# Storing two tiles of a matmul's output: SyncE's six partitions move to GpSimd, and the transfers are cut anew

## Chip, cores and metric

The kernel runs on one core of one Trainium2 chip. The metric is the device time of the kernel in microseconds; the time before is the median of three runs. The core moves data with 16 DMA engines. SyncE (SP) and GpSimd (POOL) each have a queue of transfers to them: in the profile q1, "hardware_dynamic", is SyncE's and q0, "software_dynamic", is GpSimd's.

## What is computed

```python
x          (16, 512, 1024) float32
weight     (1024, 768)     float32
scale      0.1
add_value  (16, 512, 768)  float32
out = (scale * np.matmul(x, weight) + add_value).astype(np.float32)
```

Flattened, that is 8192 rows of x against one weight matrix.

## The kernel before

The 8192 rows are cut into 64 tiles of 128 rows, four blocks of `R = 16`. A block has 2048 consecutive rows, 16 to each partition, so tile t of a block is row t of each partition. A run of n neighbouring tiles of a block is then n x 3072 consecutive bytes per partition of the output, and a transfer of it has one long packet per partition.

- **SyncE** (`sync_engine`) issues the transfers of a list written out by hand, `STREAM`, in its order: "w" loads the weight, "x" loads tiles of x into the 16 places of `xs`, "a" loads tiles of add_value into the 32 places of `ao`, "o" stores tiles from `ao`. Ahead of an entry it waits for what the entry needs (`need`): a load into a place that has been used waits for that place to be free, a store waits on `made`, VectorE's count of finished tiles. Later entries wait behind an entry that waits. The very last store, tiles 60 to 63, stands at the end of the kernel.
- **ScalarE and GpSimd** (`mover`) cast x to bf16, each half of the partitions, and lay it out in `va`.
- **VectorE** (`vector_engine`) casts the weight once, transposes `va` into `xt` and finishes two tiles at a time: `ao = scale * mm + ao`.
- **TensorE** multiplies tile by tile, eight weight pieces for each, into PSUM (`mm`).

Tiles 8 and 15 of the first block are stored apart from their neighbours. The stream stores tiles 0 to 7 with ("o", 0, 8) and 9 to 14 with ("o", 9, 6). The pair, places 8 and 15 of `ao` (`PAIR`, a slice with step 7), is stored by `store_pair`, which takes a range of partitions and has two rows of 3072 bytes for each. The 128 partitions are divided: SyncE's entry ("pair", 8, 8) stores the six in `BY_SP`; GpSimd stores the others in three transfers, `BY_POOL`, between its second and third turn over the 16 places of `xs`, once tile 15 is made. `TURN_AT` places that between two loops of casts.

Tiles 40 to 47 of add_value are loaded over places 8 to 15, so SyncE's "a" entry for them, line 129, waits for both parts of the pair: `pair_sem` for SyncE's transfer, `aside_sem` for GpSimd's three, each counting 16 to a transfer. Behind that entry in the stream stand x 48 to 55 (line 116) and the stores of tiles 16 to 31 (line 147). Line 93 is the transfer in `store_pair`, line 258 the last store.

Of the kernel before, what the change touches and what calls it, by code (L numbers as in the profile page):

```python
# [21 lines left out]
STREAM = [  # L22
# [5 lines left out]
]  # L28
FIRST, LAST = (0, 8), (60, 4)
PAIR, TURN_AT = slice(8, 16, 7), 2  # L30
BY_SP, BY_POOL = [(122, 6)], [(117, 5), (0, 105), (105, 12)]


@with_exitstack
def kernel(
# [8 lines left out]
    nc = tc.nc  # L44
# [14 lines left out]
    out_v = out_f.rearrange("(g p t) n -> p g t n", p=P, t=R)  # L59
    w_v = weight.rearrange("(c p r) n -> p c (r n)", p=P, r=2)  # L60

    def rows(view, s, n):
        assert s // R == (s + n - 1) // R
        return view[:, s // R, s % R:s % R + n, :]
# [5 lines left out]
    ao = const.tile([P, A_SLOTS, N], fp32, name="ao")  # L70
# [6 lines left out]
    x_sem = [tc.alloc_semaphore(f"x{i}") for i in range(X_SLOTS // MOVE)]  # L77
    a_sem = tc.alloc_semaphore("a")
    o_sem = [tc.alloc_semaphore(f"o{i}") for i in range(2)]
    pair_sem, aside_sem = (tc.alloc_semaphore(name) for name in ("pair", "aside"))  # L80
    by_act, by_pool, pool_go, turned, casts, done, made = (
        tc.alloc_semaphore(name)
        for name in ("by_act", "by_pool", "pool_go", "turned", "casts", "done", "made"))
# [1 line left out]
    MADE = TURNED + 2 + MM_BUFS - 2  # L85
    W_AT = A_SLOTS - KJ

    def slot(t):
        return t % A_SLOTS

    def store_pair(eng, p, n, sem):
        assert PAIR.stop <= R and PAIR.stop <= A_SLOTS
        eng.dma_start(out_v[p:p + n, 0, PAIR, :], ao[p:p + n, PAIR, :]).then_inc(sem, 16)  # L93

    def sync_engine(eng):
        groups, stores, known = 0, [], {}

        def need(sem, value):
            if known.get(sem, 0) < value:
                eng.wait_ge(sem, value)  # L100
                known[sem] = value

        for at, (op, s, n) in enumerate(STREAM):
            if at == SYNC_AT:
                eng.addr_align(HALF_BLOCK, offset=PAST, max_nops=0)
            last = s + n - 1
            if op == "w":
                dst = ao[:, W_AT + s:W_AT + s + n, :].rearrange("p (c r) n -> p c (r n)", r=2)
                move, sem = eng.dma_start(dst, w_v[:, s // 2:(s + n) // 2, :]), w_sem[s // 4]
            elif op == "x":  # L110
                k = s % X_SLOTS
                if last >= X_SLOTS:
                    moved = 8 * (last + 1 - X_SLOTS) // MOVE
                    need(by_act, moved)
                    need(by_pool, moved)
                move = eng.dma_start(xs[:, k:k + n, :], rows(x_v, s, n))  # L116
                sem = x_sem[k // MOVE]
            elif op == "a":
                if groups:
                    need(a_sem, 16 * groups)  # L120
                if last == A_SLOTS - 1:
                    need(casts, KJ)
                if s <= PAIR.start + A_SLOTS <= last:
                    need(pair_sem, 16 * len(BY_SP))
                    need(aside_sem, 16 * len(BY_POOL))
                if s >= A_SLOTS:
                    i = next(j for j, (a, b) in enumerate(stores) if a <= last - 1 - A_SLOTS < a + b)
                    need(o_sem[i % 2], 16 * (i // 2 + 1))
                move = eng.dma_start(ao[:, slot(s):slot(s) + n, :], rows(add_v, s, n))  # L129
                sem = a_sem  # L130
                groups += 1
            elif op == "pair":
                need(made, MADE + last + 1)
                for p, n in BY_SP:
                    store_pair(eng, p, n, pair_sem)
                continue
            elif op == "a+":
                need(a_sem, 16 * groups)
                eng.sem_inc(a_sem, 16 * (n // G - 1))
                groups += n // G - 1  # L140
                continue
            else:
                i = len(stores)
                if i > 1:
                    need(o_sem[i % 2], 16 * (i // 2))
                need(made, MADE + last + 1)
                move = eng.dma_start(rows(out_v, s, n), ao[:, slot(s):slot(s) + n, :])
                sem = o_sem[i % 2]
                stores.append((s, n))
            move.then_inc(sem, 16)  # L150
            if op == "x" and n == 2 * MOVE:
                eng.sem_inc(x_sem[k // MOVE + 1], 16)

    def mover(eng, copy, parity, count, go=None, first=0, turns=T // X_SLOTS):
        if go is None:
            eng.preload_act_table(mybir.ActivationFunctionType.Copy)  # L156
        with eng.Fori(16 * (first + 1), 16 * (first + turns) + 1, 16) as i:
            for q in range(X_SLOTS // MOVE):
                eng.wait_ge(x_sem[q], i)
                eng.wait_ge(turned, i + (4 * q - 12) if q < 3 else i)  # L160
                if go is not None:
                    eng.sem_inc(go, 1)  # L162
                k = MOVE * q
                src = xs[:, k:k + MOVE, :].rearrange("p i (c b k) -> p (i c) b k", b=4, k=64)
                for a in (parity, parity + 2):
                    for b in range(4):
                        copy(va[q % VA_BUFS][32 * b:32 * b + 32, :, a, :],  # L167
                             src[32 * a:32 * a + 32, :, b, :]).then_inc(count, 1)

    def vector_engine(eng):  # L170
        ao_g = ao.rearrange("p (g t) n -> p g t n", t=G)

        def cast_w(s, n):
            eng.wait_ge(w_sem[s // 4], 16)
            eng.tensor_copy(w_bf[:, s:s + n, :], ao[:, W_AT + s:W_AT + s + n, :]).then_inc(casts, n)  # L175

        def turn(move, half, moves=None):
            if half == 0:
                eng.wait_ge(by_act, moves)
                eng.wait_ge(by_pool, moves)  # L180
            q = 2 * half * KC
            eng.transpose(  # L182
                xt[:, 2 * half:2 * half + 2, :, :].rearrange("p i c m -> p (i c m)"),
                va[move % VA_BUFS][:, q:q + 2 * KC, :, :].bitcast(fp32).rearrange("p c a k -> p (c a k)"),
            ).then_inc(turned, 2)

        def finish(pair, at, products):
            eng.wait_ge(done, products)
            a = ao_g[:, at, 2 * pair:2 * pair + 2, :]
            q = 2 * (pair % 2)  # L190
            eng.scalar_tensor_tensor(  # L191
                a, mm[:, q:q + 2, 0:N], float(scale), a,
                op0=mybir.AluOpType.mult, op1=mybir.AluOpType.add).then_inc(made, 2)

        def group(i, at, last):
            eng.wait_ge(a_sem, i)
            for p in range(4):
                finish(p, at, i + (4 * p - 12) if p < 3 else i)
                if p < 2 or not last:
                    turn(1 if p < 2 else 0, p % 2, i + 8 if p == 2 else i)  # L200

        cast_w(0, 4)
        cast_w(4, 4)
        turn(0, 0, 8)
        turn(0, 1)
        with eng.Fori(16, 2 * T, 16) as i:
            group(i, bass.ds((i // 16 + A_SLOTS // G - 1) % (A_SLOTS // G), 1), False)
        s = slot(T - G) // G
        group(2 * T, slice(s, s + 1), True)
# [31 lines left out]
    s, n = FIRST  # L241
# [4 lines left out]
    with tc.tile_critical(no_gpsimd_drain=True):  # L246
        sync_engine(nc.sync)
        mover(nc.scalar, nc.scalar.copy, 0, by_act)
        mover(nc.gpsimd, nc.gpsimd.tensor_copy, 1, by_pool, pool_go, 0, TURN_AT)
        nc.gpsimd.wait_ge(made, MADE + PAIR.stop)  # L250
        for p, n in BY_POOL:
            store_pair(nc.gpsimd, p, n, aside_sem)
        nc.gpsimd.addr_align(HALF_BLOCK, offset=PAST, max_nops=0)
        mover(nc.gpsimd, nc.gpsimd.tensor_copy, 1, by_pool, pool_go, TURN_AT, T // X_SLOTS - TURN_AT)
        vector_engine(nc.vector)
        tensor_engine(nc.tensor)
    s, n = LAST
# [36 lines left out]
```

## Time and profile before

| what | value |
|---|---|
| time, median of 3 runs | 208.54 us (208.38 to 208.83) |
| the profiled execution: its time | 208.3 us |
| the profiled execution: its span | 206.5 us |
| granted TensorE clock | 0.985 |
| TensorE busy | 167.6 us, 81% |
| GpSimd busy | 137.7 us, 67% |
| moved | 87.04 MB, mean 422 GB/s |

The span goes from the first to the last instruction of the profiled execution. The page's rows on DMA count packets: each is one piece of a transfer on one DMA engine, and a queue's share is the time of its packets over 16 DMA engines times the span. A completion, which counts up a semaphore, is a small packet of its own. The DMA view can be asked for a window of time. It then counts the packets that begin in the window, and the share is their whole time over 16 times the window, so that for a narrow window with one packet, share x 16 x window is the time of that packet.

### The profile page before, as it was taken

To read this page: it belongs to the slowest core of one execution; us is meant where nothing else is said; L and a number is where in the kernel's file an instruction comes from. 1 tells how busy PE (TensorE), PEld (TensorE's weight loads), DVE (VectorE), ACT (ScalarE), POOL (GpSimd) and SP (SyncE) were. 2 spreads that over 40 slices of the span, in tenths; PEclk is the share of its full clock that TensorE was granted. 3 is DMA by queue.
4 is the path that set the end of the run, shared out by engine and by line. 5 is a ranking of instruction groups with operands and counts; after the bars stand their busy time and mean duration, and the time that the engine had idled before them with its cause. 6 is when DMAs were issued, how large, how long until landed. Compare 5 with 4: busy or idle time off the path is not lost.

```text
span 206.5 us, 2224 instructions
## 1 busy us (share of the span) xinstructions
PE 167.6 (81%) x1008; PEld 50.4 (24%) x512; DVE 98.0 (47%) x66; ACT 134.7 (65%) x129; POOL 137.7 (67%) x135
## 2 busy tenths in 40 slices
PE   0000099999999999999999999999999997999900
PEld 0000023333322233333322333333222332333200
DVE  0004525537555555465555554655552854455320
ACT  2049980799999807999998069999990199910000
POOL 0049994699999906999999459999991199920000
PEclk9999999999999999999999999999999999999985
DMA  7989999999999999999999999999999999899995
GB/s 286 425 375 459 414 478 406 424 446 451 406 457 457 406 406 413 409 447 420 432 433 449 449 397 436 457 419 414 438 448 401 438 440 490 371 438 433 443 400 248
DMA packets 4067, 87.04 MB, mean 422 GB/s; under 512 B 476, under 2 KB 476, under 8 KB 1122
## 3 DMA queue, kind: packets, MB, share of 16 engines
q1 hardware_dynamic: 3874, 86.28, 97.7%
q0 software_dynamic: 192, 0.75, 0.9%
q14 instruction: 1, 0.01, 0.0%
HBM read 61.87 MB, written 25.17 MB: 421 GB/s over the span
## 4 chain that ended last, share of the span: by engine, by line
PE 46%; DMA 29%; POOL 9%; ACT 5%; issue 3%; DVE 3%; SPq 0%; DVEq 0%; POOLq 0%; ACTq 0%
PE mm L214 46%; DMA xs<-in_x_dram 15%; DMA out_dram<-ao 14%; POOL va L167 9%; ACT va L167 5%; DVE xt L182 2%; DVE ao L191 1%; SPq L129 0%; SPq L116 0%; DVEq L180 0%; DVEq L191 0%; SPq L100 0%; ACTq L160 0%; POOLq L162 0%; POOLq L160 0%
## 5 line engine op out<-in xcount | busy, mean ns | idle before, releaser
L214 PE MATMUL mm<-w_bf,xt 128*128 128x256 bf16 (+1 forms) x1008 | 167.6, 327 | 28.1 <-DVE xt L182 27.3
L167 POOL CAST va<-xs 32x1024 bf16<-32x1024 f32 x128 | 135.5, 1059 | 44.2 <-DMA xs<-in_x_dram 36.8
L167 ACT CAST va<-xs 32x1024 bf16<-32x1024 f32 x128 | 133.4, 1043 | 45.4 <-DMA xs<-in_x_dram 42.4
L191 DVE SCALAR_TENSOR_TENSOR ao<-mm,ao 128x1536 f32 (+1 forms) x32 | 56.2, 1757 | 73.2 <-PE mm L214 69.2
L212 PEld LDWEIGHTS <-xt 128*128 128x128 bf16 x512 | 50.4, 98 | 144.8 <-issue 116.7
L182 DVE STREAM_TRANSPOSE xt<-va 128x1024 f32<-128x1024 f32 x32 | 39.5, 1236 | 8.1 <-POOL va L167 6.0
L175 DVE CAST w_bf<-ao 128x3072 bf16<-128x3072 f32 x2 | 4.5, 2254 | 18.2 <-DMA ao<-in_weight_dram 18.2
L156 ACT ACT_TABLE_LOAD x1 | 1.3, 1283 | 1.3 <-SPq L246 1.3
L93 POOL DMA_DIRECT2D out_dram<-ao x3 | 2.0, 662 | 0.0
L275 POOL MEMSET const-float32-0.0<- 128x1 f32 x1 | 0.1, 98 | 0.2 <-issue 0.2
L275 POOL MEMSET const-bfloat16-1.0<- 128x1 bf16 x1 | 0.1, 101 | 0.0
L275 POOL MEMSET const-float32-1.0<- 128x1 f32 x1 | 0.1, 98 | 0.0
L275 POOL MEMSET const-uint8-127<- 128x1 uint8 x1 | 0.1, 98 | 0.0
## 6 DMA issues: line engine op xcount, KB each, us to landing
xs<-in_x_dram SPq DMA_DIRECT2D x7, 4096.0 KB, 21.6
ao<-in_add_value_dram SPq DMA_DIRECT2D x6, 3072.0 KB, 15.9
out_dram<-ao SPq DMA_DIRECT2D x3, 3072.0 KB, 28.5
ao<-in_add_value_dram SPq DMA_DIRECT2D x1, 6144.0 KB, 24.2
out_dram<-ao SPq DMA_DIRECT2D x1, 6144.0 KB, 31.2
out_dram<-ao SPq DMA_DIRECT2D x1, 4608.0 KB, 14.7
xs<-in_x_dram SPq DMA_DIRECT2D x2, 2048.0 KB, 21.0
ao<-in_weight_dram SPq DMA_DIRECT2D x2, 1536.0 KB, 17.0
```

The source lines that it names most:

```text
L93: eng.dma_start(out_v[p:p + n, 0, PAIR, :], ao[p:p + n, PAIR, :]).then_inc(sem, 16)
L156: eng.preload_act_table(mybir.ActivationFunctionType.Copy)
L167: copy(va[q % VA_BUFS][32 * b:32 * b + 32, :, a, :], src[32 * a:32 * a + 32, :, b, :]).then_inc(count, 1)
L175: eng.tensor_copy(w_bf[:, s:s + n, :], ao[:, W_AT + s:W_AT + s + n, :]).then_inc(casts, n)
L182: eng.transpose(xt[:, 2 * half:2 * half + 2, :, :].rearrange("p i c m -> p (i c m)"), va[move % VA_BUFS][:, q:q + 2 * KC, :, :].bitcast(fp ...
L191: eng.scalar_tensor_tensor(a, mm[:, q:q + 2, 0:N], float(scale), a, op0=mybir.AluOpType.mult, op1=mybir.AluOpType.add).then_inc(made, 2)
L212: eng.ldweights(x_j, tile_position=(0, 0))
L214: m = eng.add_instruction(mybir.InstMatmult(start_tensor_calc=(j == 0), stop_tensor_calc=(j == KJ - 1), tile_size=(P, P), tile_position=(0 ...
L275: nc = _bacc.Bacc("TRN2", target_bir_lowering=False, num_devices=1)
```

## The change

SyncE's entry for the pair is taken out of the stream, and with it `BY_SP`, `pair_sem`, the branch for "pair" in `sync_engine` and one of the two waits ahead of the load of tiles 40 to 47. GpSimd stores all 128 partitions of the pair, again in three transfers at the same place of its program: partitions 122 to 127, then 0 to 97, then 98 to 121. Before, it had 117 to 121, 0 to 104 and 105 to 116.

```diff
-    ("x", 32, 8), ("a+", 16, 16), ("o", 0, 8), ("o", 9, 6), ("pair", 8, 8), ("a", 32, 8), ("x", 40, 8),
+    ("x", 32, 8), ("a+", 16, 16), ("o", 0, 8), ("o", 9, 6), ("a", 32, 8), ("x", 40, 8),
...
-BY_SP, BY_POOL = [(122, 6)], [(117, 5), (0, 105), (105, 12)]
+BY_POOL = [(122, 6), (0, 98), (98, 24)]
...
-    pair_sem, aside_sem = (tc.alloc_semaphore(name) for name in ("pair", "aside"))
+    aside_sem = tc.alloc_semaphore("aside")
...
-    def store_pair(eng, p, n, sem):
+    def store_pair(eng, p, n):
...
-        eng.dma_start(out_v[p:p + n, 0, PAIR, :], ao[p:p + n, PAIR, :]).then_inc(sem, 16)
+        eng.dma_start(out_v[p:p + n, 0, PAIR, :], ao[p:p + n, PAIR, :]).then_inc(aside_sem, 16)
...
                 if s <= PAIR.start + A_SLOTS <= last:
-                    need(pair_sem, 16 * len(BY_SP))
                     need(aside_sem, 16 * len(BY_POOL))
...
-            elif op == "pair":
-                need(made, MADE + last + 1)
-                for p, n in BY_SP:
-                    store_pair(eng, p, n, pair_sem)
-                continue
...
         for p, n in BY_POOL:
-            store_pair(nc.gpsimd, p, n, aside_sem)
+            store_pair(nc.gpsimd, p, n)
```

## The prediction

> **What bounds the kernel now.** I read the page first, its DMA lines before its engine lines.
>
> ```profile
> span 206.5 us, 2224 instructions
> PE 167.6 (81%) x1008; PEld 50.4 (24%) x512; DVE 98.0 (47%) x66; ACT 134.7 (65%) x129; POOL 137.7 (67%) x135
> ...
> DMA  7989999999999999999999999999999999899995
> ...
> q1 hardware_dynamic: 3874, 86.28, 97.7%
> q0 software_dynamic: 192, 0.75, 0.9%
> ```
>
> The two queues keep the 16 DMA engines busy for 98.6% of the span, and no slice between the first and the last falls under 8. The view of stretches says the same of the part after the pair of tiles, and the timeline shows that the last compute step leaves the queue fed:
>
> ```profile
> 109.00:204.00 95.00, 85.18 (x517) 25.63 (x262) 47.41 (x33) 53.95 (x52) 56.35 (x55) 0.98 1.00 432
> ```
> ```profile
> 195.82 1.76 DVE L191 SCALAR_TENSOR_TENSOR ao<-mm,ao 128x1536 f32<-128x1536 f32 x1 [3.44 <-PE mm L214]
> 197.87 0.33 SPq L258 DMA_DIRECT2D out_dram<-ao  x1
> ```
> ```profile
> q1 hardware_dynamic: 30, 1.11, 106.6%
> ```
>
> The DMA share is 1.00 from 109 to 204, and the third fence (DMA view, 198.0 to 200.4) shows full engines after the final store has been issued. PE's 46% in the chain of waits is therefore only how the chain was followed back. The end is set by the DMA engine that has most work, and a few rows moved from one DMA engine to another can show. So I asked the DMA view for narrow windows. At the end, for 204.06:206.5, 204.65:206.5, 204.70:204.73, 204.87:204.89 and 205.14:205.16 in that order:
>
> ```profile
> DMA packets 25, 0.11 MB, mean 45 GB/s; under 512 B 16, under 2 KB 16, under 8 KB 16
> DMA packets 5, 0.01 MB, mean 7 GB/s; under 512 B 4, under 2 KB 4, under 8 KB 4
> DMA packets 2, 0.00 MB, mean 0 GB/s; under 512 B 2, under 2 KB 2, under 8 KB 2
> DMA packets 1, 0.00 MB, mean 0 GB/s; under 512 B 1, under 2 KB 1, under 8 KB 1
> DMA packets 1, 0.00 MB, mean 0 GB/s; under 512 B 1, under 2 KB 1, under 8 KB 1
> ```
>
> The packets under 512 B are the completions, one per DMA engine. Twelve come from 204.06 to 204.65, two at 204.72, one at 204.88 and one, which ends the kernel, at 205.15. All the unevenness that a redistribution can remove is the 0.4 us between the last and the pair behind it.
>
> **Which DMA engines carry the pair of tiles.** A partition's two rows are 6144 bytes, one packet on GpSimd's queue. Its time, from 103.49:103.51, is 146.2% x 16 x 20 ns / 2 = 234 ns:
>
> ```profile
> q0 software_dynamic: 2, 0.01, 146.2%
> ```
>
> How GpSimd's transfers are spread is told by the 192 packets of the page: 122 partitions, 3 x 16 = 48 completions, and 22 left over. I read those as fillers for DMA engines without a row. Five rows on five leave 11; 105 as 15 times 7 leave one DMA engine with 7; 12 on twelve leave 4. That is 22. The windows 104:108 and 112.3:112.9 agree:
>
> ```profile
> DMA packets 107, 1.62 MB, mean 406 GB/s; under 512 B 5, under 2 KB 5, under 8 KB 53
> DMA packets 18, 0.41 MB, mean 676 GB/s; under 512 B 4, under 2 KB 4, under 8 KB 6
> q0 software_dynamic: 6, 0.01, 5.2%
> ```
>
> Five fillers in 4 us come from one DMA engine whose other packets last 0.91 us; four stand together where the 12-partition transfer runs. Who they are I got by following every DMA engine's packets, the end of one to the start of the next. The DMA engine with seven fillers is also one of the five of the first transfer and one of SP's six; here it takes a row from GpSimd (101.065:101.075, 150.6% x 16 x 10 ns = 241 ns) and, at that one's end, a 3072-byte packet of SP's (101.305:101.31, 124 ns):
>
> ```profile
> q0 software_dynamic: 1, 0.01, 150.6%
> q1 hardware_dynamic: 1, 0.00, 155.0%
> ```
>
> So the transfers take consecutive DMA engines, each going on where the last stopped, and 5 + 15 + 12 = 32 is two full turns. With E0 for the first one used: SP's 6 on E0 to E5, then 5 on E0 to E4, 105 on E5 to E15 and E0 to E3, 12 on E4 to E15. The Trainium skill (DMA: Bandwidth & Descriptors, section "Why a DMA increments its semaphore by 16 and not by 1") gives this as a rule: the largest count up to 16 that divides the partitions, consecutive from a round-robin cursor on the software queue, the lowest-numbered on the hardware queue. By that rule, the trace agrees, with its 22 fillers.
>
> New transfers, by the same reading: 6 on E0 to E5, 98 as 14 times 7 on E6 to E15 and E0 to E3, 24 as 12 times 2 on E4 to E15; 6 + 14 + 12 = 32 again. Partitions per DMA engine, both tiles' rows counted together:
> - E0 to E3: 1 + 1 + 7 + 0 = 9 before; 1 + 7 + 0 = 8 after.
> - E4: 1 + 1 + 0 + 1 = 3 before; 1 + 0 + 2 = 3 after.
> - E5: 1 + 0 + 7 + 1 = 9 before; 1 + 0 + 2 = 3 after.
> - E6 to E15: 0 + 0 + 7 + 1 = 8 before; 0 + 7 + 2 = 9 after.
>
> Both sum to 128. No byte is added.
>
> **Why each DMA engine ends where it does.** Two are special. One fetches instructions: in 98.54:98.545 a packet of 386.2% x 16 x 5 = 309 ns, and the packet beside it (98.84:98.85) lasts 543.1% x 16 x 10 = 869 ns where its like (99.79:99.80) lasts 686.
>
> ```profile
> q14 instruction: 1, 0.01, 386.2%
> q1 hardware_dynamic: 1, 0.02, 543.1%
> q1 hardware_dynamic: 1, 0.02, 428.8%
> ```
>
> Its packets lead to the last completion, at 205.15, and it is one of E0 to E3. The other is E4, slow at big stores from SBUF: in 94.28:94.30 its packet lasts 299.7% x 16 x 20 = 959 ns where another's (94.38:94.39) lasts 570.0% x 16 x 10 = 912.
>
> ```profile
> q1 hardware_dynamic: 1, 0.02, 299.7%
> q1 hardware_dynamic: 1, 0.02, 570.0%
> ```
>
> It repeats that in every large store and, despite its 3 partitions, is the one at 204.88. The two at 204.72 are E5 and the latest of E6 to E15.
>
> **The change, part by part.**
>
> *SP's store goes.*
>
> ```profile
> 74.23 0.38 SPq L93 DMA_DIRECT2D out_dram<-ao  x1
> 95.96 0.36 SPq L129 DMA_DIRECT2D ao<-in_add_value_dram  x1
> ```
>
> It is 0.38 us of SP's time, after which SP waits for the first store anyway; nothing on the path. What counts is its data: 2 x 124 ns on E0 to E5. The wait on its semaphore ended long before GpSimd's; nothing.
>
> *The shares.* The fetching DMA engine loses one partition, 0.23 to 0.25 us: 205.15 becomes about 204.91. E4 stays at 204.88. The latest of E6 to E15 gains one: 204.72 + 0.23 = 204.95. E5 loses six: about 203.3. The new last is 204.95 instead of 205.15: **-0.20 us** on this execution. The order among the ten is set by how late each entered the pair, within the 0.6 us over which most completions lie, and need not repeat. Were the fetching DMA engine 0.25 us less late than here, the ten would have ended within 0.15 of it before, and one partition more makes +0.05 to +0.25. So the bounds are -0.25 and +0.25, the median lies near -0.1, and I take that.
>
> *GpSimd's issue.* Three before, three after:
>
> ```profile
> 96.44 1.98 POOL L93 DMA_DIRECT2D out_dram<-ao  x3
> ```
>
> The same instructions with other counts; I take no difference, within 0.1 us either way, and GpSimd's casts behind them have the data of a full queue as cover.
>
> *GpSimd's last landing, and SP's wait on it.* Behind SP's wait stand the load of tiles 40 to 47 of add_value, then x 48 to 55, and two stores.
>
> ```profile
> 114.98 0.33 SPq L129 DMA_DIRECT2D ao<-in_add_value_dram  x1
> 116.02 0.33 SPq L116 DMA_DIRECT2D xs<-in_x_dram  x1
> out_dram<-ao POOLq DMA_DIRECT2D x1, 630.0 KB, 15.0
> out_dram<-ao POOLq DMA_DIRECT2D x1, 72.0 KB, 17.0
> ```
>
> On a DMA engine, GpSimd's packets alternate with SP's. A second row per DMA engine in the last transfer is one more turn: 0.234 + the x packet between, 32 KB, which by bytes from 912 ns for 24 KB is 1.22 (estimate): 1.45 us. The landing that ended SP's wait, and with it the issue, moves from 114.98 to about 116.4. The queue then still holds x 40 to 47: of its completions (118.7:119.25, then 119.25:120.2) one comes early and 15 after 119.25.
>
> ```profile
> DMA packets 3, 0.06 MB, mean 104 GB/s; under 512 B 1, under 2 KB 1, under 8 KB 1
> DMA packets 32, 0.42 MB, mean 440 GB/s; under 512 B 15, under 2 KB 15, under 8 KB 15
> ```
>
> From an issue to its first packets I take 1.0 to 1.8 us: the kernel's first load, issued at 0.74, has its 16 first packets in 1.74:2.58.
>
> ```profile
> 0.74 0.38 SPq L243 DMA_DIRECT2D xs<-in_x_dram  x1
> ...
> q1 hardware_dynamic: 16, 0.52, 220.6%
> ```
>
> So the load is ready at 117.4 to 118.2, a microsecond before the ten run dry; E4 and E5, lighter, may wait a few tenths, which E5 has to spare. The cover is x 40 to 47; without it each microsecond of lateness costs a microsecond on all 16. I count nothing. The x load, issued at 116.02 now, follows at 116.9 and is needed 7 us later.
>
> Sum: the profiled execution took 208.3 us, span 206.5 and 1.8 around it. The median is 208.54, so this execution was 0.24 under it. 208.54 - 0.1 = **208.4 us**.
>
> **Rivals.**
>
> *Slower: the wait decides.* GpSimd's last transfer lands so late that x 40 to 47 has run out. The point is a landing at about 118.3: plus 1.2 to the first packets, the fifteen are dry at 119.5. At 119.8, 1.5 us past it, the result is 208.5 + 1.5 = 210.0. For it: GpSimd's 630 KB and 72 KB transfers took 15.0 and 17.0 us from issue to landing, and nothing shows what 98 and 24 partitions take. Against it: the landing must be 3.4 us later than I work out. 9 in 100.
>
> *Slower: another spread.* If a transfer filled the lowest-numbered DMA engines by ceilings instead, 98 would lie as 7 on E0 to E13 and 24 as 2 on E0 to E11. E4 would have 1 + 7 + 2 = 10 partitions instead of 3, 7 x 0.234 = 1.64 later, at 206.5, 1.37 after today's end: 209.9. The same section of the Trainium skill names such a spread as an exception on the software queue, of some direct copies. Against it stands the DMA engine with seven fillers, which holds rows of SP's, so it isn't the sixteenth, left out by ceilings. 6 in 100.
>
> *Faster: E5 is slow too in other executions.* If E5 lost on stores what E4 does, it would have ended about 1 us later before, and the change frees it: 207.5. Against it, no row shows it. With an unevenness that favours the change, 12 in 100.
>
> *The change moves nothing.* Same bytes, and the order of lateness happens to cancel it: 208.5. It lies within my forecast. The Trainium skill (same page, section "Issuing engines are not separate DMA queues") would expect this, since every queue uses the same 16 DMA engines. By that rule the time stays; the trace can't exclude it.
>
> **How the numbers follow.** The forecast with its bounds (208.2 to 208.8), the last rival in it, has 73 in 100. A measurement of this kernel can tell about 0.2%, 0.42 us, so it counts as the same almost whole; I leave 2 of its 73 for slower and 1 for faster. Faster 0.13, the same 0.70, slower 0.17. The range goes from 207.9, halfway to the faster rival, to 209.2, halfway to the slower ones, and leaves out some 2 in 10.
>
> **What would show it.** Right: GpSimd's queue with 128 + 48 + 10 + 14 + 8 = 208 packets and 0.79 MB, SP's with 3874 - 12 - 6 = 3856; fillers of seven on two DMA engines; SP's load of tiles 40 to 47 issued near 116.4; DMA digits of 9 there; the last completion not the fetching DMA engine's alone but a cluster near 204.95. Wrong: an issue past 118.3 with a gap in the DMA digits near 120, a single completion after 206, or a median over 0.42 us from 208.54.

## The result and the profile after

| kernel | median | lowest to highest | runs | to the kernel before, with its interval |
|---|---|---|---|---|
| before | 208.51 us | 208.18 to 208.83 | 22 | 1 |
| changed | 208.19 us | 207.98 to 208.45 | 22 | 0.9985 (0.9979 to 0.9991) |

The change takes off 0.15%, some 0.3 us. The forecast was 208.4, with "the same within 0.2%" as the likeliest case. Measured twice more beside the kernel before, the changed kernel stood at 0.9993 (0.9984 to 1.0002) and 0.9985 (0.9973 to 0.9996): small and of one sign, and in one of the three not clear of noise. The ratios and intervals leave out a run that is over 1.5% above the fastest of its kernel, and there is one such, 211.38 us in e9 below. The profiled execution took 208.1 us with a span of 206.3.

The page after, in the lines that answer to those shown of before:

```profile
span 206.3 us, 2222 instructions
...
DMA  7989999999999999999999999999999999999986
...
DMA packets 4065, 87.04 MB, mean 422 GB/s; under 512 B 480, under 2 KB 480, under 8 KB 1120
...
q1 hardware_dynamic: 3856, 86.25, 97.7%
q0 software_dynamic: 208, 0.79, 0.9%
```

SyncE's queue has the 18 packets fewer that were worked out, GpSimd's the 208. The small packets that GpSimd's queue sends to DMA engines without a row (the fillers of the prediction) agree with the new spread in the window 104:107.6 (DMA view):

```profile
DMA packets 103, 1.54 MB, mean 428 GB/s; under 512 B 8, under 2 KB 8, under 8 KB 51
```

Eight small packets in 3.6 us, where before one DMA engine gave one every 0.91 us: two DMA engines now go without the 98. The DMA view of the end, for 204.0:206.3, 204.65:206.3, 204.90:206.3 and 205.03:205.05:

```profile
DMA packets 33, 0.21 MB, mean 91 GB/s; under 512 B 16, under 2 KB 16, under 8 KB 16
DMA packets 10, 0.00 MB, mean 0 GB/s; under 512 B 10, under 2 KB 10, under 8 KB 10
DMA packets 3, 0.00 MB, mean 0 GB/s; under 512 B 3, under 2 KB 3, under 8 KB 3
DMA packets 1, 0.00 MB, mean 0 GB/s; under 512 B 1, under 2 KB 1, under 8 KB 1
```

Ten of the 16 completions now come after 204.65, where four did, yet the last is at 205.04 instead of 205.15: in this execution a broad front instead of two stragglers. The timeline has the late issue, GpSimd's stores unchanged:

```profile
96.22 2.01 POOL L93 DMA_DIRECT2D out_dram<-ao  x3
...
116.34 0.33 SPq L128 DMA_DIRECT2D ao<-in_add_value_dram  x1
116.77 0.38 SPq L116 DMA_DIRECT2D xs<-in_x_dram  x1
```

116.34 against the 116.4 that was worked out, 1.36 us later than before. This point moves from one execution to the next: in the profiled executions of the same kernel measured again it is at 115.50 (experiment e5 below) and 116.39 (e11):

```profile
115.50 0.33 SPq L128 DMA_DIRECT2D ao<-in_add_value_dram  x1
116.39 0.33 SPq L128 DMA_DIRECT2D ao<-in_add_value_dram  x1
```

### The profile page after: what moved, and what is told of

Its sections match the earlier page's. It is cut to its first block, busy times and chain, and to the rows that moved or that the text cites. A ratio compares the mean times of both kernels' runs of the same rounds, so it can differ in the third digit from the quotient of the medians.

```text
span 206.3 us, 2222 instructions
## 1 busy us (share of the span) xinstructions
PE 168.5 (82%) x1008; PEld 50.5 (24%) x512; DVE 98.0 (48%) x66; ACT 134.7 (65%) x129; POOL 137.4 (67%) x135
## 3 DMA queue, kind: packets, MB, share of 16 engines
q1 hardware_dynamic: 3856, 86.25, 97.7%
## 4 chain that ended last, share of the span: by engine, by line
DMA 37%; PE 37%; POOL 10%; ACT 5%; issue 4%; DVE 2%; SPq 1%; POOLq 0%; DVEq 0%; ACTq 0%
PE mm L208 37%; DMA out_dram<-ao 22%; DMA xs<-in_x_dram 15%; POOL va L161 9%; ACT va L161 5%; DVE xt L176 1%; DVE ao L185 1%; POOL out_dram L93 1%; SPq L128 0%; SPq L116 0%; DVEq L174 0%; SPq L100 0%; POOLq L154 0%; POOLq L151 0%; DVEq L185 0%
```

## The experiments

Times stand beside the median of the kernel before on the same chip: 208.32 us for e1 to e4, 208.42 for e5 to e7, 208.40 for e8 and e9, 208.47 for e10 to e12. Single runs of the kernel before were up to 1.3 us above it (209.75 beside e5 to e7). E0 to E15 are the DMA engines as the prediction numbers them; the trace doesn't name them.

**The same three transfers in another order (e1).**

```diff
-BY_POOL = [(122, 6), (0, 98), (98, 24)]
+BY_POOL = [(0, 98), (98, 24), (122, 6)]
```

> The three transfers of the changed kernel in another order: 98, 24, then 6 partitions; same queue, same waits, same bytes. Theory of the shares (the DMA engine with most work sets the end; a partition of the pair costs 0.234 us on the DMA engine that carries it; transfers take consecutive DMA engines from where the last stopped): 98 lies as 7 on E0 to E13, 24 as 2 on E14, E15 and E0 to E9, 6 as 1 on E10 to E15. Partitions: E0 to E9 have 9, E10 to E13 8, E14 and E15 3. E4, the slow one, has 9 instead of 3, six times 0.234 = 1.40 later: last completion near 204.88 + 1.40 = 206.3 instead of 205.04, time 208.19 + 1.24 = 209.4. Rival, the gain came from taking the store and its wait away from SyncE: those are away here too, 208.2. In the packets: 208 on GpSimd's queue again, fillers of seven on two DMA engines, and E4 is not one of them.

Measured: 209.61 us, 1.0065 (1.0053 to 1.0077). The profiled execution's DMA view, 205.11:205.12, 206.2:206.22:

```profile
DMA packets 1, 0.00 MB, mean 0 GB/s; under 512 B 1, under 2 KB 1, under 8 KB 1
q1 hardware_dynamic: 1, 0.00, 5.6%
DMA packets 1, 0.00 MB, mean 0 GB/s; under 512 B 1, under 2 KB 1, under 8 KB 1
q1 hardware_dynamic: 1, 0.00, 2.8%
```

The last completion is at 206.21 and the one before it at 205.11. One DMA engine ends a microsecond behind the rest, where 206.3 was worked out. It is the slow one: of the packets of 48 KB in the last large stores, eight in a row on one DMA engine take 1848 ns and more and all others at most 1822. The first of the eight, with the completion just ahead of it, in e1 (176.59:176.61) and in the changed kernel (175.24:175.26):

```profile
q1 hardware_dynamic: 2, 0.05, 589.7%
q1 hardware_dynamic: 2, 0.05, 593.8%
```

These are 1878 and 1891 ns beside 9 ns for the completion. The slow DMA engine comes to its last stores 1.35 us later in e1, where six partitions were worked out as 1.40. Bytes, queue, waits and the sizes of the transfers are those of the changed kernel, and SyncE's load of tiles 40 to 47 goes out at 116.44, as there within 0.1 us (116.34); only who carries what differs. Taking the store away from SyncE is not enough for the gain.

**All of the pair by GpSimd (e2) and all of it by SyncE (e3).** The first edits the changed kernel, the second the kernel before.

```diff
-BY_POOL = [(122, 6), (0, 98), (98, 24)]
+BY_POOL = [(0, 128)]
```

> GpSimd stores the whole pair in one transfer of 128 partitions. Theory of the shares: 8 partitions on each of the 16 DMA engines; E4 has 5 more than in the changed kernel, 5 x 0.234 = 1.17 later: last completion at 204.88 + 1.17 = 206.05, time 208.19 + 1.0 = 209.2. 128 + 16 = 144 packets on GpSimd's queue, no fillers. Rival, the gain came from SyncE being rid of the store: 208.2 or a little less, for GpSimd issues one transfer instead of three.

```diff
-BY_SP, BY_POOL = [(122, 6)], [(117, 5), (0, 105), (105, 12)]
+BY_SP, BY_POOL = [(0, 128)], []
```

> SyncE stores the whole pair in one transfer of 128 partitions at the place of its former entry; GpSimd stores none. The same 8 partitions on each DMA engine as with GpSimd's single transfer. Theory of the shares: the queue does not matter, 209.2, within 0.2 of the kernel in which GpSimd stores all; E4 is slow at big stores here too, though GpSimd's queue is not used at all. Rival, the queue matters (the changed kernel gained because GpSimd's queue runs beside SyncE's): slower than GpSimd's single transfer by 0.3 or more. Rival, GpSimd's queue costs (its packets alternate with SyncE's, SyncE waits for it): faster by 0.3 or more.

Measured: 209.33 us, 1.0043 (1.003 to 1.0056), and 209.30 us, 1.0045 (1.0032 to 1.0058). With equal shares the two queues give equal times. The DMA view has one completion at the end of each, e2 in 206.1:206.2 and e3 in 205.94:205.96, here in this order:

```profile
DMA packets 1, 0.00 MB, mean 0 GB/s; under 512 B 1, under 2 KB 1, under 8 KB 1
q1 hardware_dynamic: 1, 0.00, 0.6%
DMA packets 1, 0.00 MB, mean 0 GB/s; under 512 B 1, under 2 KB 1, under 8 KB 1
q1 hardware_dynamic: 1, 0.00, 2.8%
```

So E4, which has 8 here, ends at 206.1 and 205.95, where 206.05 was worked out. It is as slow when GpSimd's queue is never used, so that queue does not make it slow. Nor is it the wait: SyncE's load of tiles 40 to 47 goes out at 111.37 in e2 and 110.82 in e3, 5 us earlier than in the changed kernel, and both are slower:

```profile
111.37 0.33 SPq L128 DMA_DIRECT2D ao<-in_add_value_dram  x1
110.82 0.33 SPq L129 DMA_DIRECT2D ao<-in_add_value_dram  x1
```

The Trainium skill (DMA: Bandwidth & Descriptors, section "Issuing engines are not separate DMA queues") states that all queues use the same 16 DMA engines. By that rule, the trace agrees: 209.33 and 209.30. The cut into transfers is worth a microsecond: the changed kernel moves the same bytes in 208.19.

**The shares of before on GpSimd alone (e4).**

```diff
-BY_POOL = [(122, 6), (0, 98), (98, 24)]
+BY_POOL = [(117, 5), (0, 105), (105, 12), (122, 6)]
```

> GpSimd alone, in transfers of 5, 105, 12 and then 6 partitions: the shares of the kernel before (9 on E0 to E3 and E5, 3 on E4, 8 on the others) without SyncE's store. Theory of the shares, if each execution begins at E0: the time of the kernel before, 208.5 within 0.2, and not that of the changed kernel. If the place goes on from one execution to the next (38 is two turns and 6), E4 has its 3 only in some executions: times spread over 1 us and more, median about 209.4, and the fillers of seven stand on another DMA engine than E4. Rival, SyncE rid of the store is the gain: 208.2.

Measured: 208.97 us, 208.33 to 210.75, 1.0026 (1.0006 to 1.0046). A miss for both numbers. The fastest equal the kernel before. If the place where the transfers begin wandered from one execution to the next, by 6 DMA engines each time, E4 would have 3 partitions in one execution of eight and 8 or 9 in the others, which would put most near 209.4; one in twelve is clearly over that and five are under 208.7. But something adds up to 2 us in some executions. The timeline shows what is new, SyncE's issue is later still:

```profile
117.36 0.33 SPq L128 DMA_DIRECT2D ao<-in_add_value_dram  x1
```

In the profiled execution, 209.29, E4 comes to its last stores at 176.48, 1.25 us behind the kernel before. Followed back through its slow stores, it has a packet of x of 32 KB at 135.02 that takes 1302.5% x 16 x 10 = 2084 ns instead of 1213 (135.015:135.025):

```profile
q1 hardware_dynamic: 1, 0.03, 1302.5%
```

Of the 1.25 us this one packet makes 0.87. With five partitions more on top E4 would have been 2.0 us late.

**The changed kernel again, and twelve partitions by SyncE (e5, e6).** e5 has no edit; e6 edits the kernel before.

> The changed kernel once more, as the measure for its two neighbours here: 208.2, and 0.3 under the kernel before.

```diff
-BY_SP, BY_POOL = [(122, 6)], [(117, 5), (0, 105), (105, 12)]
+BY_SP, BY_POOL = [(116, 12)], [(110, 6), (0, 98), (98, 12)]
```

> The shares of the changed kernel, except that SyncE stores 12 partitions (1 on each of E0 to E11) and GpSimd 6, 98 and 12: E0 to E3 have 9 instead of 8, E4 and E5 3 as in the changed kernel, E6 to E11 9, E12 to E15 8. It tells which share was worth the 0.3 us. Theory: the DMA engine of E0 to E3 that fetches GpSimd's instructions is last when it has 9, so the time is that of the kernel before, 208.5 (last completion near 205.15). Rival, the gain came from E5 getting 3 instead of 9: E5 has 3 here, so 208.2.

Measured: 208.34 us, 0.9993 (0.9984 to 1.0002), and 208.44 us, 0.9996 (0.9981 to 1.0011). The times don't part the two. The trace of e6 says more, in 204.93:205.18 and 205.18:205.2:

```profile
DMA packets 0, 0.00 MB, mean 0 GB/s; under 512 B 0, under 2 KB 0, under 8 KB 0
DMA packets 1, 0.00 MB, mean 0 GB/s; under 512 B 1, under 2 KB 1, under 8 KB 1
```

One completion alone at 205.19, 0.27 behind the next, where 205.15 was worked out. In this execution, relieving E5 did not remove the straggler. That the straggler of the kernel before is the fetching DMA engine I have from following its packets, in one execution; by time it stays open which share brought the gain.

**A later issue (e7, e9).** Each adds one wait ahead of SyncE's load of tiles 40 to 47 in the changed kernel.

```diff
                     need(aside_sem, 16 * len(BY_POOL))
+                    need(made, MADE + 34)      # e7
+                    need(done, 68)             # e9
```

> The changed kernel, with one more wait ahead of SyncE's load of tiles 40 to 47: tile 33 must be finished, which is at about 119.2, so that the issue moves from 116.34 to about 119.3, past the point of my slower rival. All shares stay. Theory (the queue runs dry at 119.4 to 120.1 on fifteen DMA engines, and each microsecond without packets costs a microsecond): with 1.0 to 1.8 us from issue to first packets the ten are idle for 0.5 to 1.2 and the time is 208.7 to 209.4; with 2.5 to 3.5 us, as the changed kernel's trace suggests (E5 dry at 118.35, its next packet at 119.83, issued at 116.34), 209.9 to 210.9. Rival, that wait is covered by something else or made up later: 208.2.

> The changed kernel, with one more wait ahead of SyncE's load of tiles 40 to 47: TensorE must have finished tile 33, which is at 117.4, so that the issue is at about 117.5 instead of 116.3 (and 118.7 in the experiment with the later wait). The shares stay. Theory A, the price of lateness is idle DMA engines alone: first packets 1.0 us behind the issue, at 118.5, before the ten run dry at 119.4; nobody but E5 waits: 208.2 to 208.3. Theory B, packets are stretched when the queue runs close to empty, at once and again where the loads of x give way to stores near 136: like the four transfers of GpSimd, whose issue was at 117.36, 208.8 to 209.1, with runs spread over more than 1 us, and packets near 120 and 136 longer than 912 and 1213 ns.

Measured: e7 211.46 us, 210.8 to 212.41, 1.0153 (1.0127 to 1.018), above both ranges that were expected; e9 209.16 us, 208.17 to 211.38, and without the run at 211.38 208.91, 208.17 to 209.91, 1.0028 (1.001 to 1.0047). The issues, e7 and then e9, in the timeline:

```profile
118.70 0.33 SPq L129 DMA_DIRECT2D ao<-in_add_value_dram  x1
117.07 0.33 SPq L129 DMA_DIRECT2D ao<-in_add_value_dram  x1
```

Both came earlier than I had meant (119.3 and 117.5). By the prediction's rule for lateness past 118.3, a microsecond for each microsecond, e7's 0.4 past that point would cost 0.4; it cost 3 us. What it cost is seen in the view of stretches, 117 to 121, 121 to 136 and 136 to 138, of e7 and then of the changed kernel; the last two columns are DMA share and GB/s:

```profile
117.00:121.00 4.00, 3.95 (x26) 1.18 (x13) 2.71 (x2) 0.54 (x1) 0.40 (x1) 1.00 1.00 348
121.00:136.00 15.00, 14.95 (x93) 4.50 (x46) 8.82 (x6) 14.66 (x15) 14.16 (x15) 1.00 1.01 425
136.00:138.00 2.00, 2.00 (x14) 0.59 (x6) 0.40 (x1) 1.49 (x2) 1.94 (x2) 1.00 1.06 262
```
```profile
117.00:121.00 4.00, 3.95 (x26) 1.18 (x12) 2.91 (x2) 0.52 (x1) 0.38 (x1) 1.00 1.02 440
121.00:136.00 15.00, 14.95 (x93) 4.50 (x46) 8.80 (x6) 14.65 (x15) 14.16 (x15) 1.00 1.01 437
136.00:138.00 2.00, 2.00 (x14) 0.58 (x6) 0.00 (x0) 1.95 (x3) 1.94 (x2) 1.00 0.92 393
```

The share stays at 1.00 and more while the rate falls: in the main the DMA engines are not idle, their packets take longer. In e7's 119.66:119.68 two of 24 KB average 1171.9% x 16 x 20 / 2 = 1875 ns instead of 912:

```profile
q1 hardware_dynamic: 2, 0.05, 1171.9%
```

The same comes back at 136, where the loads of x give way to stores. e9 has the milder form. In 118.68:118.69 a packet of E4 takes 1092.5% x 16 x 10 = 1748 ns, and the last completion, E4's, is alone at 205.72 (205.3:205.71 and 205.71:205.73):

```profile
q1 hardware_dynamic: 1, 0.02, 1092.5%
...
DMA packets 0, 0.00 MB, mean 0 GB/s; under 512 B 0, under 2 KB 0, under 8 KB 0
DMA packets 1, 0.00 MB, mean 0 GB/s; under 512 B 1, under 2 KB 1, under 8 KB 1
```

0.84 too long in that packet, and 0.84 behind the 204.88 at which E4 ended before. That is theory B, and e4 fits it: its shares are those of before, its issue stands at 117.36, its E4 has the long packet shown above, and its times spread as e9's do. Why a packet is stretched, and why a second time at 136, these runs don't show.

**Three small transfers by SyncE (e8).**

```diff
-BY_SP, BY_POOL = [(122, 6)], [(117, 5), (0, 105), (105, 12)]
+BY_SP, BY_POOL = [(116, 4), (120, 4), (124, 4)], [(110, 6), (0, 98), (98, 12)]
```

> SyncE stores 12 partitions of the pair in three transfers of 4, all on E0 to E3; GpSimd stores 6, 98 and 12. Shares: E0 to E3 have 3 + 1 + 7 = 11, E4 and E5 1 + 1 = 2, E6 to E15 7 + 1 = 8. Theory, that the instruction-fetching DMA engine is one of E0 to E3 and enters the pair latest: it alone ends last, at 204.91 + 3 x 0.234 = 205.61, a bare completion some 0.5 us behind the other three of E0 to E3; time 208.2 + 0.57 = 208.8, 0.2% over the kernel before. Rival, only E4 is special and the fetch weighs nothing: E4 with 2 ends at 204.65, E0 to E3 near 204.97, the ten at 204.72: 208.1, under the changed kernel.

Measured: 210.03 us, 1.0069 (1.0048 to 1.009). A miss by 1.2 us. In 101.375:101.385 one of SyncE's 3072-byte packets takes 644.4% x 16 x 10 = 1031 ns, where 121 to 128 was usual:

```profile
q1 hardware_dynamic: 1, 0.00, 644.4%
```

Two completions come at 206.53 and 207.24, the other fourteen by 205.43. By the shares the two belong to E0 to E3, which carry the three small transfers; why they lost more than the partitions cost is not shown. It covered what was to be seen, so e8 tells nothing of the fetching DMA engine.

**x ahead of add_value (e10 on the changed kernel, e12 on the kernel before, e11 the changed kernel beside them).**

```diff
-    ("a", 40, 8), ("x", 48, 8),
+    ("x", 48, 8), ("a", 40, 8),
```

> The changed kernel with two entries of SyncE's stream exchanged: x 48 to 55, which waits for GpSimd's casts (done at 115.95), goes ahead of add_value 40 to 47, which waits for GpSimd's stores (landed near 116.3). The queue then gets its next 4 MB at 116.0 whatever the stores do, and add_value 40 to 47 lands near 137.2 instead of 127; VectorE needs it at 138.2. The shares stay. Theory (what lateness costs beyond the shares is stretched packets and DMA engines run dry, and the changed kernel stands 0.7 us from where it begins): no idle DMA engine near 119, 208.0 to 208.2, runs closer together than those of the changed kernel beside it. Rival, the changed kernel pays nothing for its late load: equal to it within 0.1. Rival, VectorE waits for the load and TensorE behind it: 208.5 or more.

> The changed kernel again, on the same chip as the exchange of the two entries: 208.2 to 208.35, that is 0.1 to 0.3 under the kernel before.

> The kernel before with the same two entries exchanged. Its GpSimd stores land at 114.9, so the load of add_value was not late there: by the theory of lateness the exchange brings nothing, 208.4 to 208.5; if the exchange is worth something in itself, it gains here what it gains in the changed kernel.

Measured: e10 208.21 us (208.04 to 208.57), 0.9985 (0.9973 to 0.9998); e11 208.23 us (208.01 to 208.68), 0.9985 (0.9973 to 0.9996); e12 208.43 us, 1.0001 (0.9987 to 1.0014). With e10 the load of x goes out at 115.86:

```profile
115.86 0.33 SPq L116 DMA_DIRECT2D xs<-in_x_dram  x1
116.37 0.33 SPq L128 DMA_DIRECT2D ao<-in_add_value_dram  x1
```

Nothing is gained or lost: near 116.4 the changed kernel pays nothing that can be measured for its late load. The rival that it pays nothing holds. No version beat it; 0.02 us is no difference.

## Why the prediction was right, point by point

- **The bound.** DMA engines at work from end to end, the one that is through last sets the end: shown by e1, where an exchange of order alone moves the end by 1.2 us.
- **The spread.** Right to the packet: 208, 3856, two DMA engines with fillers of seven. These counts alone can't tell it from the spread by ceilings, which leaves as many DMA engines without a row. What tells them apart is the end: E4 with ten partitions was worked out to end at 206.5, and the last completion is at 205.04; and by ceilings the order of the transfers would not matter, which in e1 it does.
- **The price of a partition.** 0.234 us: E4 with six more ended 206.21 - 204.88 = 1.33 later in e1 than in the kernel before, 0.22 for each.
- **The sum.** The last completion moved by -0.11, for -0.20 worked out; the other 0.1 of the span's -0.2 lies behind that completion and was in no term. -0.1 was taken for the median, and -0.3, -0.1 and -0.2 were measured in the three comparisons. The kernels with the shares of before ended at 205.15 and 205.16 (e12; e4, with its long packet, at 206.11), those with the new ones at 205.04, 205.13 (e5), 205.03 (e10) and 204.83 (e11): on average 0.15 earlier, but e5 hardly. That the sum came so near is in part luck, for a change this small would also have come out as the same if the shares had been worth nothing. What the prediction had right beyond that is which DMA engine carries what and what a partition costs. That the relief of the fetching DMA engine brought the gain rests on the packets followed in one execution; e6 does not part it by time from E5's relief.
- **The landing.** 1.45 us later was worked out from the alternation of the two queues, 1.36 found; but e5's profiled execution has 0.52 (115.50), so one execution is no proof of the sum.
- **Idle DMA engines, mis-sized.** "A few tenths" was 1.48: E5 was through at 118.35, as the DMA view shows (118.34:118.36), and its next packet came at 119.83 (119.83:119.84), while E4's followed at once at 118.79:

```profile
DMA packets 2, 0.03 MB, mean 1639 GB/s; under 512 B 1, under 2 KB 1, under 8 KB 1
...
DMA packets 1, 0.02 MB, mean 2458 GB/s; under 512 B 0, under 2 KB 0, under 8 KB 0
```

  E5's relief of six partitions, 1.4 us, was spent there, which is why it does not stand out at the end. It cost nothing that shows in the time, as predicted.
- **The slower rival, mis-sized.** Its place was right, its point and its price were not: I set 118.3, and with an issue at 117.07 the time is already some 0.7 us above the changed kernel's (208.91 for 208.2). I priced lateness as idle time and left out that packets are stretched. The changed kernel stands at most 0.7 us from where it begins to cost, not 2.
- **The other spread** is refuted by the end at 205.04 and by e1, as said above; **E5 slow elsewhere** never showed.

## What to carry to other kernels

When the DMA engines are busy from end to end, ask how many bytes each one carries, not how many there are: partition counts and the order of transfers decide it, and the order alone was worth 1.2 us here. Look at the last 16 completions; a lone straggler is a share to move, a broad front is the end of that road. A transfer on which a later load waits has its price in a point of time: find that point by delaying the load on purpose, and expect it earlier than idle time alone would put it (here by over a microsecond).

## What the runs showed that I had not expected

- A queue that is refilled late does not only leave gaps. Its next packets took about twice as long (two averaged 1875 ns instead of 912), with the DMA share at 1.00, and the rate falls again 16 us later (262 for 393 GB/s).
- Of two DMA engines that ran short at nearly the same time one went on at once and the other waited 1.48 us.
- With three transfers of four partitions, 72 KB together, two DMA engines ended more than a microsecond behind the rest (206.53 and 207.24); a 3072-byte packet took up to 1031 ns.
- One DMA engine of 16 is slower at large stores (959 for 912 ns with 24 KB, 1848 ns and more for at most 1822 with 48 KB), also when GpSimd's queue carries nothing (e3).
